# Two tiles' room changed, five low parts moved to GpSimd, and three due times moved in a two-layer decoder trunk

## The chip, the cores and the metric

The kernel runs on one core of one Trainium2 chip. A time is the device time of one execution in microseconds (us). The kernel before took 1951.47 us, the median of 3 runs (1951.32 to 1952.65).

## The reference

A trunk of two layers on 1024 tokens of width 1024, in float32. Layer 0 mixes tokens with a short gated convolution, layer 1 with sliding-window attention over 128 tokens; each is followed by a SwiGLU channel mixer, with RMSNorm ahead of every part and a residual sum behind it. Cut to what matters:

```
for i in range(2):
    h = rmsnorm(x, norm_mixer[i])
    mix = short_conv_mixer(h, ...) if i == 0 else swa_sink_attention(h, ...)   # ends in "... @ w_out" / "... @ w_o"
    x = x + mix
    h = rmsnorm(x, norm_ffn[i])
    g, u = split(h @ w_gate_up)          # 1024 -> 2 x 2816
    x = x + (silu(g) * u) @ w_down       # 2816 -> 1024
```

The attention has 16 query heads and 4 key heads of width 64, an RMSNorm on every query and key head, a distance bias, and one learned sink per head.

## The kernel before, in words

**Layout.** Activations lie transposed: channels on the 128 partitions, 1024 tokens along the free dimension. Every float32 operand of a matmul is split into a high part (a rounded copy, made by ScalarE) and a low part (the rest, a subtraction on VectorE), and a product is three matmuls: high by high, high by low, low by high. Nearly every matmul is 128x128 weights against 512 columns, and every matmul loads its own stationary operand.

**SBUF.** All tiles are slots of one pool; a slot is laid out when its tag is first named, one behind the other (lines 200 to 211): first `cst` (constants, 331 words), then XS0 to XS7 and A0 to A5 (8192 bytes per partition each), two each of WR, WH and WL (4096), G0 to G11 (4096, but G2 has 16 words more, 4160 bytes, since the attention keeps its softmax exponents there: 2 x 4 x 129 words), s0 and s1 (2048), X0 to X7 (4096), and then small tiles that are named later. So all large slots but G2 are whole multiples of 2048 bytes, and what lies behind G2 (G3 to G11, s0, s1, X) starts 64 bytes further, counted in 2048s, than what lies ahead of it (XS, A, WR, WH, WL, G0, G1, G2).

**The large products.** The projections of the convolution and both channel mixers work on blocks with seven products for eight (Strassen's scheme). Their weights come in granules of four 128x128 tiles: a raw granule is loaded, split into one of eight slots G0 to G7, used by 12 matmuls, and its slot goes back to the ring (`ring_granule`; the ring is made at line 985, in the order G3 to G7, G0 to G2). The matmuls of these granules are lines 918, 919 and 921: the weights in a G slot are the stationary operand, the activations in XS and A slots the moving one. The output projections (`tail_part`, lines 1035 to 1037) take their weights from WH (high parts) and WL (low parts). In the attention's projections (lines 1595 to 1597) the activations in XS are stationary, and the weights move: for the queries from A slots (k below 4) and X slots (k from 4 on).

**The order.** The order of every engine's instructions is written out by hand: `Line.work` puts a piece of TensorE work on a time line and advances it, `Line.at(t, f)` lets step f be issued when the line reaches time t. These times set only the order within each engine's queue; at run time an engine takes its queue in order and waits on semaphores.

**The attention stage** runs in 32 units (`unit(u)`). With s the planned start of a unit and e the end of its scores, its steps are: scores (PE, 1800), `sink` (GpSimd, 1822), `merge` and `bias` (VectorE, 1810 and 1817; `bias` writes the tile that `sink` wrote), `least` (1830), `exponents` (ScalarE, 1836), `inverse` (1841), `normal` (GpSimd, 1845); a unit later `turn` (PE, 1851), `turn_hi` and `turn_lo` (1859, 1863), `select` (GpSimd, 1867); then `values` (PE, 1886), `o_copy`, `o_add` (1900, 1904), `o_hi` and `o_lo` (ScalarE 1913, GpSimd 1917). Between them run the next queries (`q_square` to `q_lo`; `q_lo` is GpSimd, 1761; `q_turn` is PE, 1767; `q_keep` is ScalarE, 1772) and keys and values (`kv_v_hi`, `kv_v_lo`, `kv_square` 1664, `kv_sum` 1677 and 1619, `kv_guess` 1623 and 1626, `kv_scale`; `key_turn` is PE, 1701; `key_hi` ScalarE 1705, `key_lo` VectorE 1710). `key_turn` and `q_turn` use the same PSUM bank, so each waits until the other's result has been copied out. The steps of keys are in the units with odd u whose query half n = u // 2 is odd and below 12.

From unit 24 on, free places on TensorE are filled with the first half of the output projection (`tail_part(0, m, ...)`). Its weights are prepared by `tail_weights`: load, high part on ScalarE (line 857), low part. For the first five of them (`early`) the low part is made in two halves of 512 columns on VectorE (line 1008). What is to be stored goes out through GpSimd's queue (line 1062).

Of the kernel before, what the change touches and what calls it, by code (L numbers as in the profile page):

```python
# [13 lines left out]
ALU = mybir.AluOpType  # L14

P = 128
D = 1024
# [24 lines left out]
C_ID = C_ONES + 1  # L42
C_OWN = C_ID + P
C_END = C_OWN + P


WARM = 9
# [22 lines left out]
def trunk_kernel(ctx: ExitStack, tc: tile.TileContext, xT, small, table, w_in, w_out, w_kv, w_q, w_o, w_gu, w_dn, out):  # L70
# [3 lines left out]
    dve, act, pool, pe = nc.vector, nc.scalar, nc.gpsimd, nc.tensor  # L74
# [3 lines left out]
    def slot(tag, shape=(P, D), dtype=F32, bufs=1):  # L78
        uid[0] += 1
        return sb.tile(list(shape), dtype, tag=tag, name=f"{tag}_{uid[0]}", bufs=bufs)  # L80
# [11 lines left out]
    def plain(ap):  # L92
        return ap.bitcast(F32)
# [103 lines left out]
            dve.tensor_tensor(out_t[:, c], src, in1[:, c], ALU.mult)  # L197


    cst = slot("cst", (P, C_END))  # L200
    nc.scalar.dma_start(cst[:, :C_SINK], small[:, :C_SINK])

    for tag in [f"XS{k}" for k in range(NK)] + [f"A{k}" for k in range(6)]:
        pair_slot(tag)
    for tag in ("WR", "WH", "WL"):
        slot(tag, bufs=2)
    for tag in [f"G{k}" for k in range(12)]:
        slot(tag, (P, D + 16) if tag == "G2" else (P, D))
    for tag in ("s0", "s1"):
        slot(tag, (P, HALF))  # L210
    X = [slot(f"X{k}") for k in range(NK)]

    ident = cst[:, C_ID : C_ID + P]
    ones = cst[:, C_ONES : C_ONES + 1]
# [5 lines left out]
    def finish_x(stage, m, first, hi_eng=act, ss_eng=pool, parts=1):  # L220
# [6 lines left out]
        for c in cs:  # L227
            if hi_eng is act:
                act.activation(xs[:, 0, c], X[m][:, c], AF.Copy, scale=g)
            else:  # L230
                hi_eng.tensor_scalar(xs[:, 0, c], X[m][:, c], g, None, ALU.mult)
        for c in cs:
            dve.scalar_tensor_tensor(xs[:, 1, c], X[m][:, c], g, plain(xs[:, 0, c]), ALU.mult, ALU.subtract)
        if first:
            state["ss"] = slot("G1")
            act.activation(state["ss"], X[m], AF.Square)
        else:
            sq = slot(("G2", "G11")[m % 2])
            act.activation(sq, X[m], AF.Square)
            ss_eng.tensor_tensor(state["ss"], state["ss"], sq, ALU.add)  # L240
# [52 lines left out]
    def add_x(m, ps):  # L293
        for src, c in ps.parts:
            dve.tensor_tensor(X[m][:, c], src, X[m][:, c], ALU.add)

# [471 lines left out]
    class Line:  # L768
# [8 lines left out]
        def at(self, t, f, *args):  # L777
            self.n += 1
            heapq.heappush(self.heap, (t, self.n, f, args))
# [75 lines left out]
    def split_steps(out_hi, out_lo, raw, lo_eng=dve):  # L855
        return (
            lambda: act.copy(out_hi, raw),  # L857
            lambda: lo_eng.tensor_tensor(out_lo, raw, plain(out_hi), ALU.subtract),  # L858
        )
# [118 lines left out]
    def channel_mixer(layer, next_stage, src_of, operands, raw_tags, extra_tags, slots, line, lead_in):  # L978

        at = line.at  # L980
        n_op = NK
# [9 lines left out]
        def tail_weights(h, m, t):  # L991
            it = {}
            c = slice(0, n_op * P)
            early = layer == 1 and h == 0 and m < 5

            def load():
                it["w"] = Weights()
                it["w"].load(src_of(m), 0, n_op)

            def hi():  # L1000
                it["w"].alloc()
                it["steps"] = split_steps(it["w"].hi[:, c], it["w"].lo[:, c], it["w"].raw[:, c])
                it["steps"][0]()

            def lo(i):
                h = slice(i * n_op * P // 2, (i + 1) * n_op * P // 2)
                w = it["w"]
                dve.tensor_tensor(w.lo[:, h], w.raw[:, h], plain(w.hi)[:, h], ALU.subtract)

            at(t - (17.0 if early else 14.0), load)  # L1010
            at(t - (8.2 if early else 5.2), hi)
            if early:
                at(t - 5.6, lo, 0)
                at(t - 3.9, lo, 1)
            else:
                at(t - 4.2, lambda: it["steps"][1]())
            return lambda: (it["w"].hi, it["w"].lo)
# [113 lines left out]
        for u in range(GROUP):  # L1131
            if whole:
                t = (origin + 4.0, origin + 12.0, begin1 + 1.0, begin1 + 8.0)[u]
# [12 lines left out]
        t = begin1 + 6.2  # L1146
        for odd in (0, 1):
            if odd and whole:
                t = begin1 + 28.0
# [5 lines left out]
        t = begin2 + 6.2  # L1155
# [30 lines left out]
        t = begin2 + 20.5  # L1186
# [292 lines left out]
        for k in range(1, KINDS):  # L1479
            if k == KINDS - 1 and next_stage is not None:  # L1480
                t = line.end
# [13 lines left out]
    def attention_layer(line, mixer):  # L1495
        at = line.at
# [423 lines left out]
        def lead_in(tail_part, tail_item):  # L1920
# [3 lines left out]
            t = line.end  # L1924
# [62 lines left out]
            def tail_piece():  # L1987
                m, k = tails.pop()
                if k + 1 < NK:
                    tail_part(0, m, [k])  # L1990
                else:
                    tail_item(0, m, k)
# [6 lines left out]
            def unit(u, last):  # L1999

                s = line.end
                begins.append(s)
                n, g = u // 2, u % 2
                b, c = n // 2, n % 2
                todo = deque(fill[u] if u < NU else [])

                def next_piece():
                    if todo:
                        f, *args = todo.popleft()
                        f(*args)  # L2010
                    elif u >= NU:
                        tail_piece()

                if u < NU:
                    line.work(8 * (small_mm + (0.12 if b else 0.0)), scores, u)
                    e = line.end
                    at(s + 0.3, sink, u)
                    for j in (0, 1):
                        if b:
                            at(e + 0.05 + 0.85 * j, merge, u, j)  # L2020
                        at(e + 0.5 + 0.85 * j, bias, u, j)
                    if b == 0:
                        at(e + 1.5, blank, u)
                    at(e + 1.8, least, u)
                    at(e + 2.65, exponents, u)
                    at(e + 4.75, inverse, u)
                    at(e + 5.0, normal, u)
                    if g == 0:
                        kb = (b, 1) if c == 0 else (b + 1, 0)
                        if 0 < kb[0] < NB:  # L2030
                            turn_keys(*kb, e + 0.3, e + 2.4)
                if 0 <= u - 2 < NU:
                    pb = (u - 2) // 4
                    line.work(4 if pb else 2, values, u - 2)
                    at(line.end + 0.05, o_copy, u - 2)
                    at(max(line.end + 0.7, s + 3.6), o_add, u - 2)
                    if g == 1:
                        at(s + 6.95, o_hi, n - 1)
                        at(s + 7.9, o_lo, n - 1)
                for _ in range(3 if u == NU else 1):  # L2040
                    next_piece()
                if 0 <= u - 1 < NU:
                    line.work(4 * small_turn, turn, u - 1)
                    at(line.end + 0.05, turn_hi, u - 1)
                    at(max(line.end + 0.7, s + 4.2), turn_lo, u - 1)
                    if u - 1 >= 4:
                        at(line.end + 0.75, select, u - 1, 0)
                        at(max(line.end + 1.4, s + 4.95), select, u - 1, 1)
                if u >= NU:
                    for _ in range(6):  # L2050
                        next_piece()
                    return
                for i in range(5):
                    next_piece()
                    if i == (1 if g == 0 else 0) and n + 1 < 16:
                        turn_query(n + 1, g, s + 5.8)
                if n + 2 < 16 and g == 0:
                    m = n + 2
                    for d, f in (
                        (5.75, q_square),  # L2060
                        (6.35, q_sum),
                        (7.2, q_guess),
                        (6.8 + 3.4, q_newton),
                        (6.8 + 5.2, q_scale),
                        (6.8 + 6.2, q_hi),
                        (6.8 + 7.3, q_lo),
                    ):
                        at(s + d, f, m)
                if g == 1 and n < 12 and n % 2:
                    kb = n // 2 + 2  # L2070
                    for d, f in (
                        (3.57, kv_v_hi),
                        (5.0, kv_v_lo),
                        (5.7, kv_square),
                        (6.1, kv_sum),
                        (6.9, kv_guess),
                        (6.8 + 3.5, kv_scale),
                    ):
                        at(s + d, f, kb)
                if g == 0 and c == 1 and b + 1 < NB:  # L2080
                    at(s + 3.5, dv_sum, b + 1)
                    at(s + 8.0, dv_hi, b + 1)
                    at(s + 8.4, dv_lo, b + 1)
# [57 lines left out]
def _small(inp):  # L2141
# [6 lines left out]

    c = np.zeros((P, C_END), f)
    gains = [inp["norm_mixer"][0], inp["norm_ffn"][0], inp["norm_mixer"][1], inp["norm_ffn"][1]]  # L2150
# [62 lines left out]
```

## Time and profile before

| what | value |
|---|---|
| the profiled execution | 1951.75 us |
| its span, first to last instruction | 1950.0 us |
| TensorE busy | 1937.1 us, 8681 matmuls |
| VectorE, ScalarE, GpSimd busy | 1389.9, 855.8, 282.5 us |
| DMA | 325.28 MB, 167 GB/s on the mean |
| mean granted TensorE clock | 0.999 |

How to read it: times in the trace are microseconds from the span's start; "mean ns" is the length of one instruction. Matmuls are pipelined: one begins before the last has ended, so their busy times overlap and TensorE's 99% doesn't say how fast they follow each other. That is read from their starts, or from their number in a stretch. PE is TensorE, PEld its load of the stationary operand, DVE VectorE, ACT ScalarE, POOL GpSimd. Groups are named by line and by the tiles written and read ("G<-WR"), without the number of the slot.

### The profile page before, as it was taken

How to read it: one execution, taken by the hardware profiler on the slowest of the kernel's cores; microseconds unless marked ns; L12 is line 12 of the kernel's file. 1: busy time of each engine (PE TensorE's matmuls, PEld its weight loads, DVE VectorE, ACT ScalarE, POOL GpSimd, SP SyncE). 2: the span in 40 equal slices, each digit the busy share in tenths (PEclk: the TensorE clock that was granted, in tenths of full speed). 3: DMA queues.
4: the chain of work that ended last, by engine and by line, in shares of the span. 5: the costliest groups of instructions: out<-in, count | busy, mean ns of one | idle time of the engine just before them, and what ended most of it. 6: DMA issues, size and time to landing. Idle time of an engine off the chain costs nothing.

```text
span 1950.0 us, 24687 instructions
## 1 busy us (share of the span) xinstructions
PE 1937.1 (99%) x8681; PEld 1581.5 (81%) x8681; DVE 1389.9 (71%) x2362; ACT 855.8 (44%) x1703; POOL 282.5 (14%) x442
## 2 busy tenths in 40 slices
PE   9999999999999999999999998999999999999999
PEld 7888888888888888888888887887888888888887
DVE  8997777866676767665768888678767676765543
ACT  5543444523333334443656766545333333344441
POOL 0000011011111111000015666400111111110000
PEclk9999999999999999999999999999999999999999
DMA  8522185245545437986620003424444554477562
GB/s 313 165 97 76 59 295 207 67 152 192 177 168 205 166 137 261 333 302 221 226 66 1 1 23 130 153 107 128 158 166 164 205 177 168 152 278 258 196 221 101
DMA packets 146764, 325.28 MB, mean 167 GB/s; under 512 B 14288, under 2 KB 54352, under 8 KB 146512
## 3 DMA queue, kind: packets, MB, share of 16 engines
q1 hardware_dynamic: 122592, 239.26, 36.5%
q0 software_dynamic: 23904, 84.42, 11.4%
q8 instruction: 68, 1.11, 0.2%
q14 instruction: 56, 0.46, 0.1%
q10 hardware_dynamic: 144, 0.03, 0.0%
HBM read 228.76 MB, written 94.90 MB: 166 GB/s over the span
## 4 chain that ended last, share of the span: by engine, by line
PE 94%; DVE 3%; POOL 1%; issue 1%; ACT 0%; DMA 0%; SPq 0%; POOLq 0%; DVEq 0%
PE acc L921 16%; PE acc L919 16%; PE acc L918 16%; PE P L919 9%; PE P L918 9%; PE P L921 9%; PE acc L1037 2%; PE acc L1035 2%; PE acc L1036 2%; PE P L1597 2%; PE P L1595 2%; PE P L1596 2%; PE acc L1800 1%; PE acc L1886 1%; PE acc L157 1%
## 5 line engine op out<-in xcount | busy, mean ns | idle before, releaser
L921 PE MATMUL acc<-XS,G 128*128 128x512 f32 x880 | 346.5, 394 | 0.0
L919 PE MATMUL acc<-XS,G 128*128 128x512 f32 x880 | 346.5, 394 | 0.0
L918 PE MATMUL acc<-XS,G 128*128 128x512 f32 x880 | 346.4, 394 | 0.0
L919 PEld LDWEIGHTS acc<-XS,G 128*128 128x128 f32 x880 | 165.3, 188 | 38.4
L918 PEld LDWEIGHTS acc<-XS,G 128*128 128x128 f32 x880 | 165.4, 188 | 38.2
L921 PEld LDWEIGHTS acc<-XS,G 128*128 128x128 f32 x880 | 165.3, 188 | 38.2
L918 PE MATMUL P<-A,G 128*128 128x512 f32 x476 | 187.2, 393 | 0.6 <-DVE G L1244 0.6
L921 PE MATMUL P<-A,G 128*128 128x512 f32 x476 | 187.3, 394 | 0.0
L919 PE MATMUL P<-A,G 128*128 128x512 f32 x476 | 187.3, 394 | 0.0
L918 PE MATMUL acc<-A,G 128*128 128x512 f32 x440 | 173.4, 394 | 0.0
L921 PE MATMUL acc<-A,G 128*128 128x512 f32 x440 | 173.2, 394 | 0.0
L919 PE MATMUL acc<-A,G 128*128 128x512 f32 x440 | 173.2, 394 | 0.0
L858 DVE TENSOR_TENSOR G<-WL,G 128x512 fp32r<-128x512 f32 x168 | 114.9, 685 | 57.0 <-ACT G L857 57.0
L857 ACT CAST G<-WR 128x512 fp32r<-128x512 f32 (+1 forms) x200 | 121.0, 605 | 66.2 <-PE acc L921 31.8
L858 DVE TENSOR_TENSOR G<-WR,G 128x512 fp32r<-128x512 f32 (+1 forms) x200 | 133.2, 666 | 12.1 <-ACT G L857 11.2
L857 ACT CAST G<-WH 128x512 fp32r<-128x512 f32 (+1 forms) x158 | 94.8, 600 | 86.9 <-PE acc L921 44.4
L1206 ACT ACTIVATE G<-G 128x512 f32<-128x512 f32 x88 | 55.8, 634 | 166.2 <-DVE G L1277 162.1
L921 PE MATMUL P<-XS,G 128*128 128x512 f32 x316 | 124.4, 394 | 0.0
L919 PE MATMUL P<-XS,G 128*128 128x512 f32 x316 | 124.3, 393 | 0.0
L918 PE MATMUL P<-XS,G 128*128 128x512 f32 x316 | 124.3, 393 | 0.0
L857 ACT CAST G<-WL 128x512 fp32r<-128x512 f32 x168 | 103.5, 616 | 35.8 <-DVE WL L801 31.8
L858 DVE TENSOR_TENSOR G<-WH,G 128x512 fp32r<-128x512 f32 (+1 forms) x158 | 104.4, 660 | 6.5 <-ACT G L857 6.4
(305 smaller groups left out, 3847.1 us busy)
## 6 DMA issues: line engine op xcount, KB each, us to landing
G<-h SPq DMA_DIRECT2D x70, 512.0 KB, 5.3
h<-X POOLq DMA_DIRECT2D x44, 512.0 KB, 5.4
X<-in_w_dn SPq DMA_DIRECT2D x80, 256.0 KB, 3.5
s<-X POOLq DMA_DIRECT2D x40, 512.0 KB, 4.4
WR<-in_w_gu SPq DMA_DIRECT2D x36, 512.0 KB, 6.1
WH<-in_w_gu SPq DMA_DIRECT2D x36, 512.0 KB, 6.2
h<-X POOLq DMA_DIRECT2D x66, 256.0 KB, 4.3
WR<-s SPq DMA_DIRECT2D x54, 256.0 KB, 3.3
```

The costliest lines, as they stand in the source:

```text
L857: lambda: act.copy(out_hi, raw),
L858: lambda: lo_eng.tensor_tensor(out_lo, raw, plain(out_hi), ALU.subtract),
L918: pe.matmul(ps, w[:, 0, c], x[:, 0, :], start=start and e == 0, stop=False, skip_group_check=True)
L919: pe.matmul(ps, w[:, 0, c], x[:, 1, :], start=False, stop=False, skip_group_check=True)
L921: pe.matmul(ps, w[:, 1, c], x[:, 0, :], start=False, stop=last, skip_group_check=True)
L1035: pe.matmul(ps, hi[:, kc], xs[:, 0, c], start=k == 0, stop=False, skip_group_check=True)
L1036: pe.matmul(ps, hi[:, kc], xs[:, 1, c], start=False, stop=False, skip_group_check=True)
L1037: pe.matmul(ps, lo[:, kc], xs[:, 0, c], start=False, stop=k == n_op - 1, skip_group_check=True)
L1206: state["silu"] = act.activation(x, x, AF.Silu)
L1595: pe.matmul(ps, x[:, 0, t], hi, start=k == 0, stop=False)
L1596: pe.matmul(ps, x[:, 0, t], lo, start=False, stop=False)
L1597: pe.matmul(ps, x[:, 1, t], hi, start=False, stop=k == NK - 1)
```

## The change

Three edits:
- `cst` gets room for 496 words, of which 331 are used as before, and G2 is laid out behind X7. So every large slot from XS0 to X7 is a whole multiple of 2048 bytes; XS0 itself starts about 640 bytes further on than before.
- The low parts of the five early output weights go from VectorE, in two halves of 512 columns, to GpSimd, in four quarters of 256 columns, due 6.4, 5.3, 4.2 and 3.1 us ahead of the first use instead of 5.6 and 3.9.
- In the units with steps of keys, `kv_square` is due at s + 6.0 instead of 5.7, `kv_sum` at s + 6.5 instead of 6.1, `kv_guess` at s + 7.2 instead of 6.9. In these units a `q_keep` is due at s + 5.8 and an `o_hi` at s + 6.95, both on ScalarE.

```diff
+C_ROOM = 496
...
-    cst = slot("cst", (P, C_END))
+    cst = slot("cst", (P, C_ROOM))[:, 0:C_END]
...
-    for tag in [f"G{k}" for k in range(12)]:
-        slot(tag, (P, D + 16) if tag == "G2" else (P, D))
+    for tag in [f"G{k}" for k in range(12) if k != 2]:
+        slot(tag)
     for tag in ("s0", "s1"):
         slot(tag, (P, HALF))
     X = [slot(f"X{k}") for k in range(NK)]
+    slot("G2", (P, D + 16))
...
             def lo(i):
-                h = slice(i * n_op * P // 2, (i + 1) * n_op * P // 2)
+                h = slice(i * n_op * P // 4, (i + 1) * n_op * P // 4)
                 w = it["w"]
-                dve.tensor_tensor(w.lo[:, h], w.raw[:, h], plain(w.hi)[:, h], ALU.subtract)
+                pool.tensor_tensor(w.lo[:, h], w.raw[:, h], plain(w.hi)[:, h], ALU.subtract)
...
             if early:
-                at(t - 5.6, lo, 0)
-                at(t - 3.9, lo, 1)
+                for i in range(4):
+                    at(t - 6.4 + 1.1 * i, lo, i)
...
                         (3.57, kv_v_hi),
                         (5.0, kv_v_lo),
-                        (5.7, kv_square),
-                        (6.1, kv_sum),
-                        (6.9, kv_guess),
+                        (6.0, kv_square),
+                        (6.5, kv_sum),
+                        (7.2, kv_guess),
                         (6.8 + 3.5, kv_scale),
```

## The prediction

> **What bounds the kernel now.** I read the page first, then the groups by line and form, then TensorE's number of matmuls in chosen stretches and its timeline, and last its waits.
>
> ```profile
> span 1950.0 us, 24687 instructions
> PE 1937.1 (99%) x8681; PEld 1581.5 (81%) x8681; DVE 1389.9 (71%) x2362; ACT 855.8 (44%) x1703; POOL 282.5 (14%) x442
> PE 94%; DVE 3%; POOL 1%; issue 1%; ACT 0%; DMA 0%; SPq 0%; POOLq 0%; DVEq 0%
> L921 PE MATMUL acc<-XS,G 128*128 128x512 f32 x880 | 346.5, 394 | 0.0
> L921 PE MATMUL P<-A,G 128*128 128x512 f32 x476 | 187.3, 394 | 0.0
> L921 PE MATMUL acc<-A,G 128*128 128x512 f32 x440 | 173.2, 394 | 0.0
> L921 PE MATMUL P<-XS,G 128*128 128x512 f32 x316 | 124.4, 394 | 0.0
> L918 PE MATMUL acc<-XS,XS 128*128 128x512 f32 x16 | 6.2, 389 | 0.0
> ```
>
> TensorE is never out of work, and the chain that ended last is TensorE's. So the time is the number of matmuls times the distance from one start to the next, plus the few holes. The granules' matmuls are the bulk: lines 918, 919 and 921 have the same counts, so 3 x (880 + 476 + 440 + 316) = 6336 with weights in G slots. The few with weights in XS last 389 ns, not 394. What counts is the distance of starts, so I counted matmuls in long stretches. A matmul that only reaches into a stretch is counted too, which adds 0.39 us to the length.
>
> ```profile
> 60.00:220.00 160.00, 160.00 (x693) 1.00 0.28 92
> 254.00:294.00 40.00, 40.00 (x178) 1.00 0.88 319
> 400.00:900.00 500.00, 500.00 (x2163) 1.00 0.60 209
> 1400.00:1900.00 500.00, 500.00 (x2163) 1.00 0.57 199
> ```
>
> With weights in G slots: 500.39 / 2163 = 231.3 ns in both channel mixers, 160.39 / 693 = 231.4 in the convolution. With weights in WH and WL (254 to 294): 40.39 / 178 = 226.9. The columns, the clock (1.00) and the work per matmul are the same, and the faster stretch has the busier DMA (0.88). The place where one stretch turns into the other is sharpest in the attention's first projections, where the stationary tile stays in XS and only the moving one changes from A to X:
>
> ```profile
> 992.87 0.39 PE L1595 MATMUL P<-A,XS 128*128 128x512 f32 x1
> 993.55 0.39 PE L1595 MATMUL P<-A,XS 128*128 128x512 f32 x1
> 994.23 0.40 PE L1595 MATMUL P<-X,XS 128*128 128x512 f32 x1
> 994.93 0.39 PE L1595 MATMUL P<-X,XS 128*128 128x512 f32 x1
> 995.62 0.39 PE L1595 MATMUL P<-X,XS 128*128 128x512 f32 x1
> ...
> ```
>
> Three matmuls lie between two of these rows: (994.23 - 992.87) / 6 = 226.7 ns with A, (995.62 - 994.23) / 6 = 231.7 with X. By the code, XS, A, WR, WH and WL lie ahead of G2, X and G3 to G7 behind it, 64 bytes off in multiples of 2048. So every fast pair has both operands on one side of G2, and slow pairs have them on two. G0 to G2 share the side of XS and A, G3 to G7 don't: five of the ring's eight slots make a slow pair, and 231.3 is a mix of (3 x 226.7 + 5 x 234.1) / 8. That the address does it is inferred: the profile shows no addresses.
>
> The holes that the other two edits can reach are TensorE's waits, all in the attention:
>
> ```profile
> PE P L1767 <- DVE G L1710: 5.1, 2, 3.6
> PE P L1701 <- ACT G L1772: 1.0, 2, 0.8
> ```
>
> **The change part by part.**
>
> *The layout.* It removes the 64 bytes between the sides: all of XS to X7 become equal in multiples of 2048. If that is what counts, every granule runs at 226.7 ns, and 6336 x (231.3 - 226.7) = 29.1 us go; with 226.9 as the fast end it is 27.9, with 226.3 (5 ns off 231.3, as 394 is off 389) 31.7. Beside them the 192 matmuls with X moving (three lines of 64) lose 5 ns each, 1.0 us, and I estimate 1.0 us more for the attention's values and the first projections, which also pair tiles of two sides. Sum: -31.1 us. The other engines must follow a TensorE that is 2% faster: VectorE, the busiest, has 71%, and no wait of TensorE lies in these stretches, so the cover holds. The cost of the move itself is nothing: no instruction or DMA is added, and `cst` keeps its own place. Transfers land 64 bytes elsewhere; the stretch at 0.88 shows DMA with room even there.
>
> The Trainium skill speaks against this part: SBUF — State Buffer, "Who interferes with whom", gives TensorE two independent read ports, one for the moving operand and one for LDWEIGHTS, and says that it never waits on anyone. By that rule the layout is worth 0. The rows at 994.23 disagree: there the pace changes as the moving tile does.
>
> *The low parts.* Removed from VectorE: ten subtractions.
>
> ```profile
> L1008 DVE TENSOR_TENSOR WL<-WR,WH x10: 679/858/3321, 1175.0 to 1229.2; 128x512 fp32r<-128x512 f32 x10
> 1176.45 1.06 DVE L1008 TENSOR_TENSOR WL<-WR,WH 128x512 fp32r<-128x512 f32 x1
> 1179.58 0.63 PE L1767 MATMUL P<-cst,G 128*128 128x128 f32 x4 [1.53 <-DVE G L1710]
> ...
> 1206.06 1.29 POOL L1761 TENSOR_TENSOR G<-s,G 128x512 f32<-128x512 f32 x1
> 1206.83 3.32 DVE L1008 TENSOR_TENSOR WL<-WR,WH 128x512 fp32r<-128x512 f32 x1
> 1207.31 1.71 POOL L1917 TENSOR_TENSOR XS<-s,XS 128x128 fp32r<-128x128 f32 x4
> 1208.98 0.63 POOL L1867 TENSOR_SCALAR_AFFINE_SELECT G<-G 128x512 fp32r<-128x512 f32 x1
> 1211.59 0.48 DVE L1710 SCALAR_TENSOR_TENSOR G<-P,qkg,G 128x256 fp32r<-128x256 f32 x1
> 1212.21 0.63 PE L1767 MATMUL P<-cst,G 128*128 128x128 f32 x4 [3.61 <-DVE G L1710]
> ...
> 1212.20:1216.00 3.80, 3.79 (x13) 3.09 (x14) 2.74 (x5) 3.03 (x10) 1.77 (x3) 0.60 0.15 59
> ```
>
> Alone such a subtraction takes 0.68 us; the one at 1206.83 took 3.32, and ends 0.5 us behind the last of six GpSimd instructions that follow each other without a gap. `key_lo` (1710) stood behind it, so the PSUM bank came free late and `q_turn` waited 3.61 us; behind the hole the granted clock was 0.60 over 3.8 us, another 1.5 us. Without line 1008 on VectorE both holes lose their cause: 1.53 + 3.61 + 1.5 = 6.6 us to be had.
>
> Added to GpSimd: 20 subtractions of 256 columns. The nearest row has the same form:
>
> ```profile
> L1726 POOL TENSOR_TENSOR G<-G,G 128x256 fp32r<-128x256 f32 x7 | 5.2, 741 | 1.8 <-ACT G L1722 1.8
> 1197.83 1.04 POOL L1845 TENSOR_TENSOR G<-G,at_d 128x512 f32<-128x512 f32 x1
> 1198.81 0.19 POOL L1822 COPY G<-cst 128x4 f32<-128x4 f32 x1
> 1198.94 0.64 PE L1851 MATMUL acc<-cst,G 128*128 128x128 f32 x4
> 1199.03 0.42 DVE L1817 TENSOR_TENSOR G<-acc,A 128x256 f32<-128x256 f32 x1 [1.33 <-POOL G L1822]
> ```
>
> At 0.741 us, one weight's four quarters are 3.0 us of GpSimd's queue, all five 14.8. Each quarter waits for ScalarE's high part, due 1.8 us earlier. By the due times the quarters come in ahead of `normal` (1845), `sink` (1822), `q_lo` (1761), `o_lo` (1917), `select` (1867), `dv_lo` and the stores (1062). There is little room: at 1198.94 `turn` began 0.07 us behind `normal`, and at 1199.03 `bias`, with VectorE's whole queue behind it, had waited 1.33 us for `sink`. The second weight puts two quarters (1.48) ahead of that `normal`; I let it cost 0.6 on TensorE, as GpSimd is no longer held by line 1008 there. For the first and third weight `sink` comes two quarters later, which `bias`, `least` and `key_lo` inherit; VectorE has 1.7 and 5.3 us of subtractions less ahead of them. I take 0.7 and 1.2 us of `q_turn`'s wait as left. New holes: 2.5 us, an estimate between 0 and all 14.8. Net -4.1 us.
>
> *The three due times.* One hole has this cause:
>
> ```profile
> 1033.19 0.37 ACT L1664 ACTIVATE P<-P 128x256 f32<-128x256 f32 x1 [0.55 <-DVE G L1671]
> 1033.47 0.59 ACT L1772 CAST G<-P 128x512 fp32r<-128x512 f32 x1
> 1034.11 0.44 PE L1701 MATMUL P<-cst,G 128*128 128x128 f32 x2 [0.76 <-ACT G L1772]
> ```
>
> ScalarE held `q_keep` behind `kv_square`, which waited for VectorE. Now `q_keep` goes first and gains 0.55 + 0.28 us: the 0.76 goes. `kv_guess` falls behind `o_hi` on ScalarE, `kv_sum` moves past nothing on VectorE; `kv_scale`, their reader, keeps its due time 3.1 us on. Without that cover it would cost the 0.3 to 0.4 us by which they are later. Net -0.8 us (bounds -0.8 and +0.4).
>
> The sum, against the profiled execution: 1951.75 - 31.1 - 4.1 - 0.8 = 1915.75. That execution lies 0.28 above the median of the runs, so the forecast is 1915.5 us.
>
> **The rivals.**
>
> *A. The layout is worth nothing*, because something else sets the 226.7 and 231.3 (the skill's rule above gives this). For it: the profile names no addresses, and slow and fast stretches differ in their stores and splits too. Against it: the switch within one kind of work at 994.23. Then 1951.5 - 4.1 - 0.8 = 1946.6; with the new holes of the low parts at twice my estimate, 1949.1. Chance 0.09, of which 0.05 is faster by over 0.2%.
>
> *B. It is the place itself that counts, not that two operands agree* (the slower side). Fast pairs were seen only on the side of XS, and the move takes all tiles to a third place. If a stationary tile there is slow, the 3/8 of the granules that are fast now go to 234.1: 6336 x (234.1 - 231.3) = 17.7 us, and some 770 matmuls of the output projections lose 7.4 ns each, 5.7 us. 1951.5 + 23.4 - 4.9 = 1970.0 us. It decides from a mean above 231.3 on. Against it: the X tiles moving against XS were slow although XS had not moved. Chance 0.05.
>
> *C. The layout pays, but GpSimd becomes the attention's bound*: all 14.8 us of quarters show on TensorE, and two holes are long enough for the clock, 3.0 us. For it: the 0.07 and the 1.33 us. Against it: from the fourth weight on no `q_lo` is left in the queue. 1951.5 - 31.1 - 0.8 - 6.6 + 17.8 = 1930.8 us. Chance 0.06.
>
> **How the numbers follow.** The forecast has 0.80, and A, B and C 0.20 together. Its own ends are 1951.5 - 33.7 - 6.6 - 0.8 = 1910.4 (fast end of the layout, no new hole), and about 1924; up to 1931 the range takes in C. A and B are left out. About 0.2%, 3.9 us, is what a measurement of this kernel can tell from no change. Faster: 0.80 + 0.06 + 0.05 = 0.91; the rest of A, 0.04, is the same; B, 0.05, is slower.
>
> **What would show it.** Right: some 2207 matmuls in a stretch of 500 us in the channel mixers instead of 2163, durations of 389 in the rows of 918 to 921, no row of 1008 on VectorE, no wait of 1767 for 1710 above 1.5 us, no granted clock below 1.00 in the attention, and 1701 without its 0.76. Wrong in the layout: 231 again, or more. Wrong in the low parts: TensorE waiting for lines 1845, 1867 or 1710 by over 6.6 us together. Anything above 1931 or below 1910 falsifies the sum.

## The result, and the profile after

| | before | after |
|---|---|---|
| median of the runs | 1951.62 us (1951.32 to 1952.65) | 1919.87 us (1919.71 to 1920.12) |
| the profiled execution, its span | 1951.75, 1950.0 us | 1919.71, 1918.0 us |

The ratio is 0.9837, with an interval of 0.9819 to 0.9854. The kernel is 31.75 us faster, and 4.4 us above the forecast of 1915.5; the time lies in the range. Lines of the kernel after stand two further on than those of before: 918 is 920, 1767 is 1769.

The page of after, lines that answer to those of before:

```profile
span 1918.0 us, 24702 instructions
...
PE 1906.7 (99%) x8681; PEld 1579.5 (82%) x8681; DVE 1380.0 (72%) x2352; ACT 855.6 (45%) x1703; POOL 292.1 (15%) x462
...
PE 92%; DVE 3%; issue 1%; POOL 1%; ACT 1%; DMA 1%; SPq 0%; POOLq 0%; DVEq 0%; ACTq 0%
...
L923 PE MATMUL acc<-XS,G 128*128 128x512 f32 x880 | 342.5, 389 | 0.0
```

The same 8681 matmuls keep TensorE at the same 99%, in 32 us less: each granule's matmul lasts 389 ns instead of 394. The busy share showed nothing of this loss before, and shows nothing of its absence now. The number of matmuls in long stretches shows it (start and end, busy time and count, granted clock, share of DMA, GB/s):

```profile
60.00:220.00 160.00, 159.91 (x706) 1.00 0.28 94
...
400.00:900.00 500.00, 500.00 (x2208) 1.00 0.63 215
1400.00:1900.00 500.00, 500.00 (x2207) 1.00 0.58 199
```

In both channel mixers 500.39 / 2208 = 226.6 ns from start to start, against 231.3, and in the convolution 160.39 / 706 = 227.2 against 231.4. The granted clock was 1.00 both times. In the attention's first projections the pace no longer changes where the moving tile does:

```profile
976.65 0.39 PE L1597 MATMUL P<-A,XS 128*128 128x512 f32 x1
...
977.33 0.39 PE L1597 MATMUL P<-X,XS 128*128 128x512 f32 x1
...
978.01 0.39 PE L1597 MATMUL P<-X,XS 128*128 128x512 f32 x1
```

From row to row it is 0.68 us, three matmuls, with A and with X; with X they took 0.69 to 0.70 before.

TensorE's waits (line and tile that waited, what it waited for: us in total, times, longest):

```profile
PE P L1769 <- DVE G L1712: 1.7, 2, 0.9
...
PE P L1703 <- ACT G L1774: 1.0, 1, 1.0
PE acc L1853 <- POOL G L1847: 0.9, 2, 0.5
...
PE acc L1888 <- POOL G L1869: 0.5, 2, 0.3
PE P L1769 <- DVE at_t L1632: 0.5, 1, 0.5
```

The long waits of `q_turn` for `key_lo` are gone (5.1 us before, 1.7 now), and the last three kinds are new. Where most of them lie, in TensorE's timeline:

```profile
1020.39 0.63 PE L1769 MATMUL P<-cst,G 128*128 128x128 f32 x4 [0.79 <-DVE G L1712]
...
1181.46 0.66 PE L1853 MATMUL acc<-cst,G 128*128 128x128 f32 x4 [0.51 <-POOL G L1847]
...
1187.94 0.44 PE L1703 MATMUL P<-cst,G 128*128 128x128 f32 x2 [1.01 <-ACT G L1774]
...
1192.72 0.52 PE L1769 MATMUL P<-cst,G 128*128 128x128 f32 x3 [0.90 <-DVE G L1712]
...
1212.01 0.66 PE L1853 MATMUL acc<-cst,G 128*128 128x128 f32 x4 [0.39 <-POOL G L1847]
...
1217.23 0.51 PE L1888 MATMUL acc<-G,G 128*128 128x512 f32 x1 [0.33 <-POOL G L1869]
```

All but the first stand beside the five early weights, whose quarters GpSimd now subtracts. VectorE's and GpSimd's rows ahead of the hole at 1187.94 show how it comes about:

```profile
1178.47 0.43 DVE L1812 COPY_PREDICATED acc<-cst,acc 128x256 f32<-128x256 int32 x1
1182.26 0.43 DVE L1819 TENSOR_TENSOR G<-acc,A 128x256 f32<-128x256 f32 x1 [3.36 <-POOL G L1824]
```

```profile
1178.38 0.73 POOL L1010 TENSOR_TENSOR WL<-WR,WH 128x256 fp32r<-128x256 f32 x1
...
1179.68 0.72 POOL L1010 TENSOR_TENSOR WL<-WR,WH 128x256 fp32r<-128x256 f32 x1
1180.37 1.03 POOL L1847 TENSOR_TENSOR G<-G,at_d 128x512 f32<-128x512 f32 x1
1181.37 0.72 POOL L1010 TENSOR_TENSOR WL<-WR,WH 128x256 fp32r<-128x256 f32 x1
1182.04 0.18 POOL L1824 COPY G<-cst 128x4 f32<-128x4 f32 x1
```

`sink` (1824), 0.18 us long, stands behind three quarters (and behind a `select` and `normal`). `bias` (1819) waits 3.36 us for it, and with it all of VectorE. `least` and the exponents come late, ScalarE's next cast begins at 1185.86, and `q_keep` behind it at 1187.33: 1.01 us late for `key_turn` (1703).

### The profile page after: what moved, and what is told of

Read it like the earlier page. It is cut to its first block, busy times and chain, and to the rows that moved or that the text cites. A ratio compares the mean times of both kernels' runs of the same rounds, so it can differ in the third digit from the quotient of the medians.

```text
span 1918.0 us, 24702 instructions
## 1 busy us (share of the span) xinstructions
PE 1906.7 (99%) x8681; PEld 1579.5 (82%) x8681; DVE 1380.0 (72%) x2352; ACT 855.6 (45%) x1703; POOL 292.1 (15%) x462
## 4 chain that ended last, share of the span: by engine, by line
PE 92%; DVE 3%; issue 1%; POOL 1%; ACT 1%; DMA 1%; SPq 0%; POOLq 0%; DVEq 0%; ACTq 0%
PE acc L920 16%; PE acc L921 16%; PE acc L923 16%; PE P L920 9%; PE P L921 9%; PE P L923 9%; PE acc L1039 2%; PE acc L1037 2%; PE acc L1038 2%; PE P L1599 2%; PE P L1597 2%; PE P L1598 2%; PE acc L158 1%; PE acc L1802 1%; PE acc L1888 1%
## 5 line engine op out<-in xcount | busy, mean ns | idle before, releaser
L920 PE MATMUL acc<-XS,G 128*128 128x512 f32 x880 | 342.7, 389 | 0.0
L923 PE MATMUL acc<-XS,G 128*128 128x512 f32 x880 | 342.5, 389 | 0.0
L921 PE MATMUL acc<-XS,G 128*128 128x512 f32 x880 | 342.5, 389 | 0.0
L920 PE MATMUL P<-A,G 128*128 128x512 f32 x476 | 185.3, 389 | 0.8 <-DVE G L1246 0.8
L923 PE MATMUL P<-A,G 128*128 128x512 f32 x476 | 185.3, 389 | 0.0
L921 PE MATMUL P<-A,G 128*128 128x512 f32 x476 | 185.2, 389 | 0.0
L920 PE MATMUL acc<-A,G 128*128 128x512 f32 x440 | 171.6, 390 | 0.0
L923 PE MATMUL acc<-A,G 128*128 128x512 f32 x440 | 171.3, 389 | 0.0
L921 PE MATMUL acc<-A,G 128*128 128x512 f32 x440 | 171.2, 389 | 0.0
L920 PE MATMUL P<-XS,G 128*128 128x512 f32 x316 | 123.1, 390 | 0.1
L921 PE MATMUL P<-XS,G 128*128 128x512 f32 x316 | 123.0, 389 | 0.0
L923 PE MATMUL P<-XS,G 128*128 128x512 f32 x316 | 123.0, 389 | 0.0
```

Source lines behind the costliest of these rows:

```text
L920: pe.matmul(ps, w[:, 0, c], x[:, 0, :], start=start and e == 0, stop=False, skip_group_check=True)
L921: pe.matmul(ps, w[:, 0, c], x[:, 1, :], start=False, stop=False, skip_group_check=True)
L923: pe.matmul(ps, w[:, 1, c], x[:, 0, :], start=False, stop=last, skip_group_check=True)
```

## The experiments

Two theories stood at the start. **Mine**: a matmul with 512 columns is slower when its two operands' addresses differ by some part of 512 bytes; what the layout is worth comes from their agreement. The low parts lose part of their gain to GpSimd's queue, and the due times only move a hole. **The rivals**: the new place of the slots or the longer room of `cst` counts; the low parts gave what the sum lacks in the layout, or the other way round. The kernel before was timed anew beside them: 1951.95 us beside the first four runs, 1952.09 beside the next three, 1951.95 beside the next four and 1952.30 beside the last. The kernel after was not: its 1919.87 us stand beside the 1951.62 of the result.

**The layout alone** (the diff's first part, and nothing else).

```diff
-    cst = slot("cst", (P, C_END))
+    cst = slot("cst", (P, C_ROOM))[:, 0:C_END]
...
+    slot("G2", (P, D + 16))
```

> The kernel before with the layout alone: room for 496 words of constants and G2 behind X7. Theory (matmuls whose stationary and moving operands lie at one place modulo 2048 bytes follow each other at 226.7 ns, others at some 233): about 2207 matmuls in 500 us of the channel mixers, the attention's holes of before (1.53, 3.61 with the clock, 0.76) still there, 1951.6 - 30.7 = 1921 us, so all but 1 or 2 us of the whole gain. Rival (part of the pace comes from taking line 1008 off VectorE, or from the order): well above 1921, with a pace above 227 ns.

Measured: 1921.88 us (1921.53 to 1921.96), 30.1 below before, ratio 0.9844 (0.9829 to 0.9858). 2208 matmuls in the stretch from 400 to 900. The holes that the low parts can reach are all still there. The fences are a line of TensorE's waits, VectorE's rows, and the stretch behind the long hole (the granted clock is the 0.58):

```profile
PE P L1769 <- DVE G L1712: 5.2, 2, 3.6
```

```profile
1186.78 1.95 DVE L1010 TENSOR_TENSOR WL<-WR,WH 128x512 fp32r<-128x512 f32 x1
...
1189.52 3.31 DVE L1010 TENSOR_TENSOR WL<-WR,WH 128x512 fp32r<-128x512 f32 x1
```

```profile
1194.90:1198.70 3.80, 3.80 (x13) 0.58 0.12 46
```

So the layout alone gives 30.1 us, and the kernel after, with the other two edits, is 2.0 us below this one. (They don't add up to 31.75, since the kernel before took 1951.95 us here and 1951.62 in the result.)

**The low parts alone.**

```diff
-                dve.tensor_tensor(w.lo[:, h], w.raw[:, h], plain(w.hi)[:, h], ALU.subtract)
+                pool.tensor_tensor(w.lo[:, h], w.raw[:, h], plain(w.hi)[:, h], ALU.subtract)
...
+                for i in range(4):
+                    at(t - 6.4 + 1.1 * i, lo, i)
```

> The kernel before with the five low parts on GpSimd alone. Theory: pace of 231.3 ns as before; the holes of 1.53 and 3.61 and the slower clock go (6.6 us), new waits of TensorE for normal, select and key_lo come (about 3.4 us in the trace of the changed kernel): 1951.6 - 3 = 1948 to 1949 us. Rival of the prediction (GpSimd becomes the bound): 1955 us or more.

Measured: 1949.95 us (1949.60 to 1950.22), 2.0 below before, ratio 0.9990 (0.9981 to 0.9999). The new waits are the same kinds as in the kernel after, so they do not come from the faster TensorE. How much of the 2.0 us is the clock, the executions of before tell. Of the 19 beside this run, four were granted a clock of 1.000 over the whole and took 1950.04 to 1950.44 us; the other fifteen had 0.998 or 0.999 and took 1951.47 to 1953.08. All ten of this kernel had 1.000. Beside the four it is only 0.3 us faster: the edit ends the fall of the clock behind the long hole, and nearly all that it takes out of the waits comes back as new ones.

**The three due times alone.**

```diff
-                        (5.7, kv_square),
-                        (6.1, kv_sum),
-                        (6.9, kv_guess),
+                        (6.0, kv_square),
+                        (6.5, kv_sum),
+                        (7.2, kv_guess),
```

> The kernel before with the three due times alone. Theory, formed on the changed kernel's trace: the hole of 0.76 us of key_turn at the fourth unit goes, but q_turn three steps on then waits for key_lo by as much, since VectorE's queue sets that time: 1951.6 us, no difference. The prediction's step: 0.8 us less, 1950.8 us, and no hole in that unit.

Measured: 1951.99 us (1951.58 to 1952.91), ratio 1.0001 (0.9991 to 1.0011): nothing. Its timeline shows why:

```profile
1033.10 0.40 PE L1701 MATMUL P<-cst,G 128*128 128x128 f32 x2
...
1036.68 0.47 DVE L1710 SCALAR_TENSOR_TENSOR G<-P,qkg,G 128x256 fp32r<-128x256 f32 x1
...
1037.30 0.63 PE L1767 MATMUL P<-cst,G 128*128 128x128 f32 x4 [0.81 <-DVE G L1710]
```

`key_turn` (1701) begins 1.0 us earlier than the 1034.11 of before and waits no more. But `key_lo` (1710) sits in VectorE's queue and comes at 1036.68, against 1036.77 before: TensorE, early now, waits 0.81 us for it at `q_turn`. The wait of 0.76 was moved by 3 us.

**The layout without the longer room of `cst`**: all large slots still a whole multiple of 2048 bytes apart, but each 640 bytes further to the front than in the kernel after.

```diff
-    cst = slot("cst", (P, C_ROOM))[:, 0:C_END]
+    cst = slot("cst", (P, C_END))
```

> The changed kernel without the longer room of the constants: G2 still behind X7, but all large slots 640 bytes lower, on the place that XS and A had before. Theory (only the agreement of the two operands counts): 226.7 ns and 1919.9 us, as the changed kernel. Rival (the third place itself is worth something, so the room is needed): slower than 1920, up to a pace above 227 ns.

Measured: 1920.11 us (1920.05 to 1920.83), ratio 0.9836 (0.9821 to 0.9851), beside 1919.87 for the kernel after. The place alone is worth nothing that these runs can tell, while all slots agree.

**How far may two operands differ?** The kernel before, with its order of slots, and only G2's room longer or shorter, so that X and G3 to G7 lie 32, 128, 512 and 256 bytes off from XS and A instead of 64.

```diff
-        slot(tag, (P, D + 16) if tag == "G2" else (P, D))
+        slot(tag, (P, D + 64) if tag == "G2" else (P, D))
```

(256 bytes; D + 8, D + 32 and D + 128 for the others.)

> The kernel before with G2 longer by 8 words instead of 16, so that G3 to G7 and X lie 32 bytes off XS, A and G0 to G2. Theory (any disagreement of the two operands costs): a mean of 231.3 ns in the channel mixers as with 64 bytes, or some value between it and 226.7. If only multiples of 64 bytes count: no telling from this alone. Rival (the offset of 64 is special): 226.7 ns, about 1921 us.

> The kernel before with G2 longer by 32 words: 128 bytes off. Theory (the two operands must agree modulo 512 bytes or more): 231.3 ns or more, about 1951 us. Rival (agreement modulo 128 bytes or less is enough): 226.7 ns, about 1921 us.

> The kernel before with G2 longer by 128 words: 512 bytes off. If agreement modulo 512 bytes is enough: 226.7 ns, about 1921 us. If it must be modulo 1024 or 2048 bytes: 231.3 ns, about 1951 us.

> The kernel before with G2 64 words longer than the others, so that X and G3 to G7 lie 256 bytes off from XS and A in multiples of 512. Theory (the two operands of a matmul have to agree modulo 512 bytes): slow, about 2170 matmuls in 500 us and 1940 to 1950 us. Rival (modulo 256 is enough): 2208 matmuls in 500 us and 1922 to 1924, as with 512.

Measured, one run each:

| bytes off | time, us | matmuls from 400 to 900 |
|---|---|---|
| 32 | 1950.44 | 2163 |
| 64 (before, beside the first three) | 1952.09 | 2163 |
| 128 | 1947.70 | 2170 |
| 256 | 1922.77 | 2208 |
| 512 | 1923.12 | 2208 |

The row of the stretch with 128 bytes, and then with 256:

```profile
400.00:900.00 500.00, 500.00 (x2170) 1.00 0.61 210
```

```profile
400.00:900.00 500.00, 500.00 (x2208) 1.00 0.63 215
```

An offset of 256 bytes, which is no multiple of 512, is as good as none in the stretch; 128 is nearly as bad as 64. So the operands have to agree modulo 256 bytes here, not 512 as I had it: that part of my theory fell. No tile was moved but by G2's room, and no instruction was changed, so the address is shown to do it, which the prediction had inferred. It is also the address of the two relative to each other: the longer room of `cst` puts every slot about 640 bytes further on, 128 more than a multiple of 256, and there G3 to G7 and X are fast in the kernel after; 128 bytes off an XS that stayed, at the same place modulo 256, they are slow. What within the chip compares them stays open.

The smaller differences in the column of times are the clock's, at least in part. With 32 bytes it stayed at 1.00 behind the attention's hole, here of 3.57 us, and the kernel is faster than with 64 without one matmul more in the stretch:

```profile
1212.40:1216.20 3.80, 3.73 (x22) 1.00 0.16 67
```

With 256 and 512 bytes it was 0.50 over the 3.80 us behind the hole, against 0.58 in the layout alone, and that is part of why they took 1922.77 and 1923.12 us and not 1921.88.

**Is GpSimd's queue full beside the early weights?** Each quarter subtracted twice, 14.8 us more in its queue.

```diff
                 pool.tensor_tensor(w.lo[:, h], w.raw[:, h], plain(w.hi)[:, h], ALU.subtract)
+                pool.tensor_tensor(w.lo[:, h], w.raw[:, h], plain(w.hi)[:, h], ALU.subtract)
```

> The changed kernel with each of GpSimd's twenty quarters subtracted twice: 14.8 us more in its queue, nothing else. Theory (in these stretches GpSimd's queue is close to full, so that more of it shows on TensorE): 1925 to 1932, with waits of TensorE for 1847, 1869 and 1712 of more than 8 us together. Rival (its idle pieces of 0.6 to 2 us take it in, and the present holes are those of other queues): 1919.9 to 1922.

Measured: 1932.00 us in one run, 12.1 above the kernel after. TensorE's waits (lines one further on than after):

```profile
PE acc L1854 <- POOL G L1848: 4.6, 4, 1.3
PE P L1770 <- DVE G L1713: 2.8, 2, 2.0
...
PE P L1704 <- ACT G L1775: 1.8, 1, 1.8
```

Of 14.8 us added, 12.1 come out at the end. Some 3.3 of them are the clock, which fell twice (0.58 over 3.8 us from 1163.40, 0.57 over 4.0 us from 1215.00: 3.8 x 0.42 + 4.0 x 0.43); the rest, as waits, is GpSimd's queue. GpSimd is busy 15% of the whole span, but in the 70 us from 1156 to 1226 it is busy for 44.77 us with the layout alone, 55.04 in the kernel after and 62.68 here: it isn't full, but some of what is left can't be used, since its queue waits there for another engine, as for VectorE over 2.24 us ahead of 1186.44 in the kernel after.

**Three weights on GpSimd, two on VectorE.**

```diff
-                pool.tensor_tensor(w.lo[:, h], w.raw[:, h], plain(w.hi)[:, h], ALU.subtract)
+                lo_eng = pool if m < 3 else dve
+                lo_eng.tensor_tensor(w.lo[:, h], w.raw[:, h], plain(w.hi)[:, h], ALU.subtract)
```

> The changed kernel, but the quarters of the fourth and fifth weight are subtracted on VectorE at the same due times; those of the first three stay on GpSimd. Theory (the holes of 0.25 to 0.5 us between 1204 and 1220 us come from GpSimd's queue, in which eight more quarters, 5.9 us, stand ahead of normal and select): they go, about 1.4 us in all, and the time is about 1918.5 (1918.0 to 1919.2); the kernel before had no wait of TensorE at these two weights. Rival (a subtraction on VectorE beside GpSimd's runs is stretched again, as the one that took 3.32 us): a wait of 1769 for 1712 or of 1853 for 1847 at these weights, and 1920 or later.

Measured: 1920.00 us (1919.63 to 1920.59), ratio 0.9836 (0.9821 to 0.9850): no gain, my expectation missed. The holes near the end are still there, with other names:

```profile
1216.21 0.74 PE L1889 MATMUL acc<-G,G 128*128 128x512 f32 x2 [0.39 <-DVE G L1866]
1217.28 0.50 PE L1889 MATMUL acc<-G,G 128*128 128x512 f32 x1 [0.33 <-POOL G L1870]
```

The eight quarters on VectorE took 0.42 us at the least, 0.59 in the median and 1.26 at the most: what GpSimd gained VectorE seems to have lost.

**`sink` on VectorE.** The first step of the chain above is `bias` waiting for `sink`; this takes that copy out of GpSimd's queue.

```diff
-            pool.tensor_copy(e_room(u)[:, :, P], cst[:, h : h + QUAD])
+            dve.tensor_copy(e_room(u)[:, :, P], cst[:, h : h + QUAD])
```

> The changed kernel with one edit more: sink, the copy of 128 x 4 numbers ahead of each unit's bias, goes from GpSimd's queue to VectorE's. Theory (what the low parts still cost is GpSimd's queue, first of all bias waiting 3.36 and 2.51 us for a sink that stands behind quarters): TensorE's waits of 1703 for 1774 (1.0 us) and of 1769 for 1712 at the second weight (0.9) go, and the time falls from 1919.9 to about 1918 (1917.4 to 1918.8). Rival (what VectorE saves in waiting is taken up by its next wait, or its 32 added copies delay it): 1919.9 within 0.4, or later, with the same waits of 1769 for 1712.

Measured: 1925.16 us (1924.93 to 1925.69), ratio 0.9863 (0.9846 to 0.9879): 5.3 us slower than the kernel after. The wait of 1703 went, as the theory had it, and a far larger one came; behind it the granted clock was 0.50 over 3.8 us, which is part of the 5.3. VectorE's row, GpSimd's (the first and the last of a run of twelve without a gap), and the hole on TensorE:

```profile
1186.13 7.64 DVE L1824 COPY G<-cst 128x4 f32<-128x4 f32 x1
```

```profile
1185.87 0.65 POOL L1869 TENSOR_SCALAR_AFFINE_SELECT G<-G 128x512 fp32r<-128x512 f32 x1
...
1193.11 0.62 POOL L1869 TENSOR_SCALAR_AFFINE_SELECT G<-G 128x512 fp32r<-128x512 f32 x1
```

```profile
1196.61 1.09 PE L1769 MATMUL P<-cst,G 128*128 128x128 f32 x4 [6.01 <-DVE G L1712]
```

A copy of four numbers per partition, 0.16 us in the median of its 32, took 7.64: from 0.26 us behind the start of GpSimd's run to 0.04 us behind its end (1193.11 + 0.62 = 1193.73, and 1186.13 + 7.64 = 1193.77).

**`sink` on ScalarE.** The same copy, on the third engine.

```diff
-            pool.tensor_copy(e_room(u)[:, :, P], cst[:, h : h + QUAD])
+            act.copy(e_room(u)[:, :, P], cst[:, h : h + QUAD])
```

> The changed kernel with sink, the copy of 128 x 4 numbers ahead of each unit's bias, on ScalarE in place of GpSimd. On VectorE this copy took 7.64 us behind a run of GpSimd's instructions without a gap, where most took 0.16. Theory (GpSimd's runs hold back copies that VectorE makes from SBUF to SBUF, and not ScalarE's): no copy on ScalarE lasts over 0.4 us, bias no longer waits for it, TensorE's waits of 1703 for 1774 (1.0 us) and of 1769 for 1712 at the second weight (0.9) go, and the time is 1917.4 to 1918.8. Rival 1 (ScalarE is held back too): copies of 1 us and more, and 1922 or later. Rival 2 (the copies come too late in ScalarE's queue, behind exponents and casts, or what they free is taken by the next wait, on turn or values): 1919.5 to 1921 without long copies.

Measured: 1915.91 us (1915.89 to 1916.03), ratio 0.9812 (0.9799 to 0.9826). This kernel beats both: 36.4 us below before, 4.0 below the kernel after, and 1.5 below the low end of what I expected (1917.4). Its 32 copies (ns: least, median, most), and TensorE's waits in the attention:

```profile
L1824 ACT COPY G<-cst x32: 180/194/211, 990.9 to 1206.4; 128x4 f32<-128x4 f32 x32
```

```profile
PE acc L1853 <- POOL G L1847: 1.0, 2, 0.5
...
PE P L1769 <- DVE G L1712: 0.8, 1, 0.8
```

None of the copies was held. The wait of 1703, the second weight's of 1769 and the two holes beside the last weights are gone; what is left of those listed for the kernel after is the hole that the due times moved (0.8) and 1.0 us for `normal`. That is 2.8 us less than there; the other 1.2 of the 4.0 us stand in none of these waits and stay open. The copy reads and writes the same tiles on all three engines, so the 7.64 us belong to VectorE beside GpSimd's run, and not to the copy's data.

## Why the prediction was right, point by point

**The forecast's case held.** Faster, in the range, by the mechanism named, with the signs that it listed: 2207 to 2208 matmuls in a stretch, 389 ns, no subtraction of 1008 on VectorE, no clock below 1.00 in these rows of the attention (from 1187.90 and from 1192.70, behind the two longest holes):

```profile
1187.90:1191.70 3.80, 3.76 (x19) 1.00 0.14 49
1192.70:1196.50 3.80, 3.78 (x23) 1.00 0.24 84
```

**The layout: -31.1 foreseen, -30.1 measured.** The granules carry it: 6336 x (231.3 - 226.6) = 29.8 us by the stretches. That leaves 0.3 us for all the rest, of which the prediction had 2.0, and 29.1 for the granules: the sum came out so near because one term was too small and the other too large. The terms that failed are the two small ones. Of X's the traces tell: by the starts, and without gaps above 260 ns, the matmuls with X moving are 231.1 ns apart on the mean before and still 230.9 with the layout alone. The 231.7 that the prediction read comes from the first six, and the 0.68 us from row to row after holds for the first twelve of them; what sets the pace of the others stays open.

What the prediction argued only from the order of slots, the offsets have shown, and the trace of before shows it within one turn of the ring. These rows are each the first of three matmuls:

```profile
703.98 0.40 PE L918 MATMUL acc<-XS,G 128*128 128x512 f32 x1
...
706.78 0.40 PE L918 MATMUL P<-A,G 128*128 128x512 f32 x1
...
720.73 0.39 PE L918 MATMUL acc<-XS,G 128*128 128x512 f32 x1
...
722.12 0.39 PE L918 MATMUL acc<-XS,G 128*128 128x512 f32 x1
...
724.84 0.39 PE L918 MATMUL acc<-XS,G 128*128 128x512 f32 x1
```

From 703.98 to 706.78 it is 2.80 / 12 = 233.3 ns, from 722.12 to 724.84 2.72 / 12 = 226.7, both with XS moving against a G slot. The pace changes in steps of whole slots: from 703.98 to 726.20 there are 36 slow, 12 fast, 24 slow and 24 fast matmuls, five slots of eight, as many as lie behind G2 by the code. But the first six behind each slow stretch are still slow, 1.39 / 6 = 231.7 ns from 720.73 to 722.12. So a slow pair is 6.6 ns slower and not 7.4, as the prediction's 234.1 would have it: (60 x 233.3 + 12 x 231.7 + 24 x 226.7) / 96 = 231.4.

The Trainium skill's rule in SBUF — State Buffer, "Who interferes with whom", has TensorE's two read ports as independent and TensorE as never waiting on anyone. What the prediction drew from it, a layout that is worth nothing, does not hold here: with the same instructions, 64 bytes between the operands cost 4.7 ns on the mean over the ring.

**The low parts: -4.1 foreseen, -2.0 measured** (alone, and as the difference of 1921.88 and 1919.87). The 6.6 us that were to be had were there: the holes of 1.55 and 3.61 and the clock of 0.58 that the layout alone still shows. The step that was mis-sized is the new holes, put at 2.5 us, which come to 6.6 - 2.0 = 4.6; 3.8 of it stand in the waits listed above for the kernel after. Of the 6.6, the clock's 1.5 stayed gained (1.7 by the executions of before), and the waits' 5.1 came back almost whole. Two parts of the step were wrong. The first: VectorE, it said, has "1.7 and 5.3 us of subtractions less ahead" of `bias`, `least` and `key_lo`, so that a later `sink` would mostly be covered. VectorE was early, and waited 3.36 us for `sink` at 1182.26 and 2.51 at 1190.24. And one path by which it reached TensorE, from the late `least` and exponents to ScalarE's `q_keep` and so to `key_turn` (1.01 us), is not in the prediction. The second: "from the fourth weight on no `q_lo` is left in the queue", so nothing was put down there; but `sink` stands behind the quarters there as well, and the rows at 1212.01 and 1217.23 are from these weights. The copy on ScalarE made the kernel 4.0 us faster, 2.8 of it in these waits: most of what the quarters cost went by way of one instruction of 0.18 us, which the prediction had named, with its 1.33 us of wait, and priced too low.

**The due times: -0.8 foreseen, 0 measured.** The step asked which wait goes and not, as it does for the other edits, what is late next. `key_lo` was 3 us behind, in VectorE's queue, at a time that ScalarE's order does not change.

**The rivals.** A and B are out by the layout alone and by the run without the longer room. C is not what happened, but its mechanism is what took the 2.1 us: one dose of quarters costs 4.6 of 14.8 us on TensorE, the second 12.1 of 14.8, with the clock's 3.3.

## What to carry to other kernels

When TensorE is never out of work, count its matmuls in long stretches of equal clock and look for a stretch that is faster: where the two differ in which buffers meet, try the addresses, which costs a line of layout. When work is moved to an engine that is idle on the mean, look at its queue in that very stretch and for short instructions with a reader whose whole queue waits; those go to a third engine first. When a hole goes behind which the clock fell, compare with those executions of the kernel before in which it didn't: that tells what the work itself gained. And for each wait that is removed, ask which queue sets the start of the next step: the 0.76 us of the due times only changed their name.

## What the runs showed of the hardware

- TensorE's start-to-start time for these matmuls with 512 columns depends on the addresses of its two operands relative to each other: 226.6 ns on the mean where all agree modulo 256 bytes, 231.3 where five slots of eight were 64 bytes off (233.3 in such a slot, 226.7 in the others, with six matmuls on the way down), 500.39 / 2170 = 230.6 with 128 bytes. It shows in no wait, no clock and no share of busy time. Only offsets of 32, 64, 128, 256 and 512 bytes were tried, and why 256 is enough stays open.
- GpSimd's instructions without a gap between them can hold one VectorE instruction through all of them: a copy of 128x4 for 7.64 us, through twelve (of the 32 such copies three were long, 0.75, 3.24 and 7.64 us; the median took 0.16). VectorE's subtractions of two SBUF tiles were held too (3.31 instead of 0.68 us). `least`, a reduction of one SBUF tile, was not (0.690 to 0.693 us in all 32 of the kernel after), nor `bias`, an addition of PSUM and SBUF (0.414 to 0.428 in all 64), nor ScalarE's copies (0.211 at most). The Trainium skill, in SBUF — State Buffer, "Who interferes with whom", has the shared port, held for the whole of one instruction; that the loser does not get it between two instructions of the other is what the row of 7.64 us adds.
- The granted clock fell to 0.58 behind a hole of 3.61 us, and stayed at 1.00 behind holes of 0.90 and 1.01. The length of the hole ahead does not settle it: with 32 bytes it stayed at 1.00 behind 3.57 us, and with the quarters doubled it was 0.58 behind a hole of 2.04 us (at 1163.42), 1.00 behind another of 2.04 (at 1199.81) and 0.57 behind one of 1.32 (at 1214.87). What does stays open. In the traces' record of the clock each of these falls is to 0.5, for 3.41 us or twice that (6.83 with 256 and 512 bytes and with `sink` on VectorE); 3.41 us at half the clock are the 1.7 us by which the executions of before differ.
